# Gated linear attention: stacked gate product, halved state product, fewer decay operations

## The chip, the cores and the metric

The kernel runs on one core of a Trainium2 chip. The metric is the device time of one execution in microseconds (us).

## What is computed

One inference step of a hybrid decoder layer: 2048 prompt tokens and 8 single-token samples, model width 1024, all float32. Each token's normalised row is projected; one part goes through sliding-window attention, the other through gated linear attention (GLA), both are joined by an output product, and a SwiGLU network follows. The change touches the GLA part, which the reference gives as

```
log_a = log_sigmoid(u_lr @ w_gla_gate2 + b_gla_gate) / 16
b = cumsum(log_a)                                       # inside a chunk
o_inter = (q * exp(b)) @ S
scores[t, s] = sum_d q[t, d] * k[s, d] * exp(b[t, d] - b[s, d])   for s <= t
o = o_inter + scores @ v
S = exp(b_last) * S + (k * exp(b_last - b)).T @ v
g = rmsnorm(o) * silu(r)
```

with four heads of 64 key and 128 value channels, and a gate of rank 16.

## The kernel before

The program has three stages on one core: projections and window attention (to about 400 us of the profile), the GLA stage (about 400 to 740 us), then the output product and the network. A scheduler, run when the kernel is built, fixes the order of the instructions on each engine by a simulated timeline; at run time every engine takes its own list in order and waits on semaphores. Edits anywhere can thus move instructions of the whole program.

In the GLA stage tokens go in eight pairs of 128-token blocks. `front_b(pp)` loads the normalised tokens of a pair and projects q and k (`ps_qk`, L685) and v (`ps_v`, L728), each as three products of a high and a low float32r part (`mm3`, L104 to L106). Its `gates()` multiplies the 16 columns of the low-rank input `lrT` with `w2` in plain float32 (`ps_g`, L706; twice a pair), then ACT and DVE make the decay and its running sum `Bt`. `gla_b(pp)` computes the scores of a pair of blocks. The decay between two tokens is split over seven levels (64, 32, 16, 8, 4, 2, 1): at each level DVE subtracts the running sum at the middle of each section from the others, once for each half of the section (L785, L786), ACT takes the exponential (L787), POOL multiplies the later halves with q into the block-diagonal tile `bd` (four operations, L802), DVE the earlier halves with k (two, L803), and PE multiplies the two (`ps_l`, L807, four float32 products of 128 columns). The result is copied into `AT` under a mask (L815; level 64 without one, by ACT, L810). Then, per block, PE forms the output `po` from `AT` and v (L854) and from the state (L857), and the state's increment `pst` (L859): keys of two heads times values of two heads, 128 by 256, of which the two 64 by 128 diagonal parts are used. DVE updates the state `Sbd` (L867) and adds the diagonal to make `ob` (L873). ACT squares (L878), POOL takes the power for the reciprocal root (`rs_r`, L112), DVE multiplies `ob` by it and by the gate `r` in four column blocks (L882), PE transposes (`ps_m`, L886), ACT evicts, and SP stores to `mix_d` (L889), from where the output product reads it.

The scheduler mixes the projections of pair pp+1 between the level products of pair pp on PE. In the last pair nothing is left to mix in but the first tiles of the output product (`ps_wo`), whose inputs come by SP's queue too. Between the attention of the last block and the first `ps_v` PE needs the first gate product; in SP's queue the loads of `lrT` stand among the stores of the attention's outputs (L391, of tile `o`). DVE also splits `wro` into `wohl` for the output product in this stage (L763).

The lines to follow: L84 to L87 (constants), L325 to L327 (`lrT` leaves the first stage), L672 to L677 and L706 (gates), L778 to L816 (levels), L848 to L867 (outputs and state), L868 to L889 (scaling).

Of the kernel before, what the change touches and what calls it, by code (L numbers as in the profile page):

```python
# [20 lines left out]
P = 128  # L21
# [30 lines left out]
def hymba_kernel(ctx: ExitStack, tc: tile.TileContext, I, O, X=None, phases=3):  # L52
# [14 lines left out]
    lr_d = [dram.tile([16, 256], F32, name=f"lr_d{i}") for i in range(NB // 2)]  # L67
# [18 lines left out]
    w2 = const.tile([16, 256], F32, name="w2")  # L86
# [57 lines left out]
    with ExitStack() as ph:  # L144
# [140 lines left out]
        def project(b):  # L285
# [39 lines left out]
            lrT = wk.tile([16, P], F32, tag="lrT", name="lrT", bufs=1)  # L325
            nc.scalar.copy(lrT, ps[:16, 2 * P:3 * P])
            nc.sync.dma_start(lr_d[b // 2][:, (b % 2) * P:(b % 2 + 1) * P], lrT)  # L327
# [206 lines left out]
        for b in range(NB):  # L534
            if b + 2 < NB:
                front(b + 2)
            if 1 < b + 1 < NB:
                project(b + 1)
                if b + 1 < NB - 2:
                    project_r(b + 1)  # L540
            attend(b)
            if b >= 1:
                next(dec, None)
            if b == 3:
                nc.sync.dma_start(gg, I["gla_norm_g"].rearrange("o d -> d o"))
                nc.sync.dma_start(w2, I["w_gla_gate2"][0])
# [39 lines left out]
    with ExitStack() as ph:  # L586
# [67 lines left out]
        for i in range(2):  # L654
            AT = pc.tile([P, 4, 2, P], F32, name=f"AT{i}")
            nc.gpsimd.memset(AT, 0.0)
            ATs.append(AT)
        for i in range(3):
            bd = bdp.tile([P, 4, 2, 64], F32, name=f"bd{i}")
# [6 lines left out]
        def front_b(pp):  # L666
# [5 lines left out]
            lrT = qkp.tile([16, 264], F32, tag="lrT", name="lrTb")  # L672
            nc.sync.dma_start(lrT[:, 0:256], lr_d[pp])
            if pp == 0:
                nc.vector.tensor_copy(nT[:, 0, :, 256:264], nTdec[:, :, 0:ND])
                nc.vector.tensor_copy(nT[:, 1, :, 256:264], nTdec[:, :, 32:40])
                nc.vector.tensor_copy(lrT[:, 256:264], lrTdec)  # L677
# [15 lines left out]
            def gates():  # L693
# [8 lines left out]
                for p in range(2):  # L702
# [3 lines left out]
                    nc.tensor.matmul(ps[:, :W], w2[:, p * P:(p + 1) * P], lrT[:, :W], start=True, stop=True)  # L706
# [65 lines left out]
        def gla_b(pp):  # L772
# [5 lines left out]
            for li, H in enumerate(LEVELS):  # L778
                J = 64 // H
                E = wl.tile([P, 2, 256], F32, tag="E", name="E", bufs=3)  # L780
                Bv = Bt.rearrange("p a (n two o) -> p (a n) two o", two=2, o=H)
                Ev = E.rearrange("p a (n two o) -> p (a n) two o", two=2, o=H)
                G = 4 * J
                ref = Bv[:, :, 0, H - 1:H].to_broadcast([P, G, H])
# [11 lines left out]
                for p in range(2):  # L796
                    bv = bd[:, 2 * p:2 * p + 2].rearrange("p g h (j o) -> p g h j o", o=H)
                    for h in range(2):
                        rows = slice(64 * h, 64 * h + 64)
                        eo = E5[rows, p, :, 1].rearrange("p (c j) o -> p c j o", c=2)  # L800
                        qo = qv[rows, p, :, 1].rearrange("p (c j) o -> p c j o", c=2)
                        nc.gpsimd.tensor_tensor(bv[rows, :, h], eo, qo, ALU.mult)  # L802
                    nc.vector.tensor_tensor(E5[:, p, :, 0], E5[:, p, :, 0], kv[:, p, :, 0], ALU.mult)  # L803
                ps = lvp.tile([P, 512], F32, tag="lv", name="ps_l")
                Ef = E.rearrange("p a t -> p (a t)")
                for g in range(4):
                    nc.tensor.matmul(ps[:, g * P:(g + 1) * P], Ef[:, g * P:(g + 1) * P],  # L807
                                     bd[:, g].rearrange("p h t -> p (h t)"), start=True, stop=True)
                if H == 64:
                    nc.scalar.copy(AT[0:64].rearrange("p g h t -> p (g h) t")[:, :, 64:128],  # L810
                                   ps[0:64].rearrange("p (g t) -> p g t", t=64))
# [6 lines left out]
            qk = wl.tile([P, 2, 256], F32, tag="E", name="qk", bufs=3)  # L818
# [12 lines left out]
            kd = wl.tile([P, 2, 256], F32, tag="E", name="kd", bufs=3)  # L831
# [12 lines left out]
            for c in range(2):  # L844
# [4 lines left out]
                for p in range(2):  # L849
# [6 lines left out]
                    if b > 0:  # L856
                        nc.tensor.matmul(po[:, p * 256:(p + 1) * 256], eBf[:, g * P:(g + 1) * P], Sbd[:, p, :],  # L857
                                         start=False, stop=last, skip_group_check=True)
                    nc.tensor.matmul(pst[:, p * 256:(p + 1) * 256], kdN[:, g, :], v[:, p * 256:(p + 1) * 256],  # L859
                                     start=True, stop=True)  # L860
                for p in range(2):
                    g = 2 * p + c
                    for h in range(2):
                        rows = slice(64 * h, 64 * h + 64)
                        hc = slice(p * 256 + h * P, p * 256 + h * P + P)
                        sl = Sbd[rows, p, h * P:(h + 1) * P]
                        nc.vector.scalar_tensor_tensor(sl, sl, ebl[rows, g:g + 1], pst[rows, hc], ALU.mult, ALU.add)  # L867
# [8 lines left out]
                for hh in range(4):  # L876
                    hc = slice(hh * P, (hh + 1) * P)
                    nc.scalar.activation(osq, ob[:, hc], AF.Square, accum_out=ss[:, hh:hh + 1])  # L878
                rr = rstd(ss, P, 1.0 / P, 4)
                for hh in range(4):  # L880
                    hc = slice(hh * P, (hh + 1) * P)
                    nc.vector.scalar_tensor_tensor(ob[:, hc], ob[:, hc], rr[:, hh:hh + 1], r[:, hc], ALU.mult, ALU.mult)  # L882
                ps = aux.tile([P, 512], F32, tag="aux", name="ps_m")
                for hh in range(4):
                    hc = slice(hh * P, (hh + 1) * P)
                    nc.tensor.transpose(ps[:, hc], ob[:, hc], ident)  # L886
# [546 lines left out]
```

## Time and profile before

| | |
|---|---|
| median of 3 runs | 2298.53 us (2294.03 to 2301.5) |
| the profiled execution, its own time | 2301.44 us |
| its span, first to last instruction | 2299.7 us |
| PE busy with matmuls | 2223.9 us, 97% of the span, 12649 records |
| DVE, ACT, POOL busy | 1597.5 us (69%), 955.6 us (42%), 627.8 us (27%) |
| mean granted clock of PE | 0.984 of full speed |

An engine's busy time is the time in which at least one of its instructions runs. The records of PE overlap: the next starts while the end of the one before is still counted, so the cost of a matmul is read from the distance between two starts. A plain float32 matmul leaves two records, a float32r one or a transpose one. "Idle before" names the wait that ended last.

### The profile page before, as it was taken

The numbers are of one execution on the slowest core, as the hardware profiler recorded it, in microseconds if no ns is written. First come the engines' busy times: TensorE is split into PE (matmuls) and PEld (weight loads), VectorE is DVE, ScalarE is ACT, GpSimd is POOL, SyncE is SP. The second block draws the span as 40 slices with busy tenths as digits, with TensorE's granted clock in tenths as the row PEclk, the third lists the DMA queues.
The fourth block names the chain that finished last, engine by engine and source line by source line (L and its number), as shares of the span: only waits on it lengthen the run. The fifth ranks groups of instructions, "written<-read, shape, count | busy, mean of one in ns | idle before, by whom it ended". The sixth has DMA issues, their size and how long they took to land.

```text
span 2299.7 us, 34866 instructions
## 1 busy us (share of the span) xinstructions
PE 2223.9 (97%) x12649; PEld 1921.5 (84%) x12649; DVE 1597.5 (69%) x3241; ACT 955.6 (42%) x2121; POOL 627.8 (27%) x799
## 2 busy tenths in 40 slices
PE   8999998899998899999999999999999999999997
PEld 6888886788887788688888889999999968787886
DVE  6787887588676466766666767666676675748487
ACT  5666777343443233423333323333333243434342
POOL 2443443455465133311110111111010122222222
PEclk9999998999998999999999999999999999999999
DMA  7323334245424699863333357323232378878777
GB/s 240 122 77 111 94 102 157 92 138 171 143 88 184 237 293 317 303 202 110 92 112 94 103 186 277 98 88 107 87 115 88 106 212 174 218 168 218 166 206 239
DMA packets 211225, 364.35 MB, mean 158 GB/s; under 512 B 15428, under 2 KB 128349, under 8 KB 207965
## 3 DMA queue, kind: packets, MB, share of 16 engines
q1 hardware_dynamic: 173996, 258.65, 34.6%
q0 software_dynamic: 37056, 103.47, 17.7%
q8 instruction: 100, 1.64, 0.3%
q14 instruction: 73, 0.59, 0.1%
HBM read 210.98 MB, written 152.16 MB: 158 GB/s over the span
## 4 chain that ended last, share of the span: by engine, by line
PE 81%; DVE 5%; DMA 5%; issue 4%; POOL 2%; ACT 2%; SPq 0%; POOLq 0%; DVEq 0%; ACTq 0%
PE ps_b L105 7%; PE ps_b L104 7%; PE ps_b L106 7%; PE ps_c L105 5%; PE ps_c L104 5%; PE ps_c L106 5%; PE ps_a L105 5%; PE ps_a L104 5%; PE ps_a L106 5%; PE ps_d L104 3%; PE ps_wo L104 3%; PE ps_d L106 3%; PE ps_d L105 3%; PE ps_wo L106 3%; PE ps_wo L105 3%
## 5 line engine op out<-in xcount | busy, mean ns | idle before, releaser
L104 PE MATMUL ps_b<-z,whl 128*128 128x258 f32 (+1 forms) x792 | 254.0, 321 | 1.2 <-ACT whl L92 1.2
L106 PE MATMUL ps_b<-z,whl 128*128 128x258 f32 (+1 forms) x792 | 253.1, 320 | 1.7 <-DVE whl L93 1.7
L105 PE MATMUL ps_b<-z,whl 128*128 128x258 f32 (+1 forms) x792 | 254.3, 321 | 0.0
L92 ACT CAST dm<-mr 128x384 fp32r<-128x384 f32 (+1 forms) x224 | 108.1, 488 | 187.2 <-PE ps_b L106 99.4
L105 PE MATMUL ps_a<-z,whl 128*128 128x258 f32 (+1 forms) x528 | 169.2, 320 | 0.0
L105 PE MATMUL ps_c<-z,whl 128*128 128x258 f32 (+1 forms) x528 | 169.1, 320 | 0.0
L106 PE MATMUL ps_a<-z,whl 128*128 128x258 f32 (+1 forms) x528 | 168.9, 320 | 0.0
L106 PE MATMUL ps_c<-z,whl 128*128 128x258 f32 (+1 forms) x528 | 168.9, 320 | 0.0
L104 PE MATMUL ps_c<-z,whl 128*128 128x258 f32 (+1 forms) x528 | 168.6, 319 | 0.2 <-DMA z<-zc_d_P 0.2
L104 PE MATMUL ps_a<-z,whl 128*128 128x258 f32 (+1 forms) x528 | 168.8, 320 | 0.0
L106 PEld LDWEIGHTS ps_b<-z,whl 128*128 128x128 f32 x792 | 149.4, 189 | 14.5 <-DVE whl L93 2.4
L104 PEld LDWEIGHTS ps_b<-z,whl 128*128 128x128 f32 x792 | 149.4, 189 | 13.1 <-ACT whl L92 1.3
L105 PEld LDWEIGHTS ps_b<-z,whl 128*128 128x128 f32 x792 | 149.3, 189 | 11.9
L93 DVE TENSOR_TENSOR dm<-mr,dm 128x384 fp32r<-128x384 f32 (+1 forms) x224 | 115.1, 518 | 59.6 <-ACT dm L92 59.6
L92 ACT CAST whl<-wrg 128x512 fp32r<-128x512 f32 x132 | 81.6, 619 | 156.7 <-PE ps_b L106 82.2
L802 POOL TENSOR_TENSOR bd<-E,qTb 64x128 f32<-64x128 f32 x224 | 126.7, 566 | 60.7 <-ACT E L787 47.2
L969 DVE TENSOR_TENSOR gu<-ps_c,gu 128x512 f32<-128x512 f32 (+1 forms) x130 | 78.0, 600 | 57.8 <-PE ps_c L106 57.2
L93 DVE TENSOR_TENSOR whl<-wrg,whl 128x512 fp32r<-128x512 f32 x132 | 90.7, 688 | 36.6 <-ACT whl L92 36.3
L1268 POOL DMA_DIRECT2D md_d<-m x22 | 15.6, 711 | 363.8 <-DVE m L1231 363.8
L92 ACT CAST whl<-sy 128x512 fp32r<-128x512 f32 x88 | 54.6, 620 | 134.7 <-PE ps_b L106 84.7
L104 PE MATMUL ps_wo<-WO,mt 128*128 128x512 f32 x256 | 103.6, 404 | 6.9 <-ACT mt L92 6.9
L104 PEld LDWEIGHTS ps_c<-z,whl 128*128 128x128 f32 x528 | 99.8, 189 | 8.6 <-issue 0.6
(390 smaller groups left out, 6669.1 us busy)
## 6 DMA issues: line engine op xcount, KB each, us to landing
mr<-md_d SPq DMA_DIRECT2D x24, 1344.0 KB
zc_d_P<-zhl POOLq DMA_DIRECT2D x56, 512.0 KB, 6.4
z<-zc_d_P SPq DMA_DIRECT2D x14, 2048.0 KB
wrg<-in_w_gate_dram SPq DMA_DIRECT2D x44, 512.0 KB
wrg<-in_w_up_dram SPq DMA_DIRECT2D x44, 512.0 KB
nT_d<-nT SPq DMA_DIRECT2D x16, 1024.0 KB
zT<-nT_d SPq DMA_DIRECT2D x8, 2048.0 KB
h_d<-gu POOLq DMA_DIRECT2D x48, 256.0 KB, 4.6
```

Of the source, the lines that this page charges most:

```text
L92: nc.scalar.copy(h, src)
L93: (eng or nc.vector).tensor_tensor(l, src, h.bitcast(F32), ALU.subtract)
L104: nc.tensor.matmul(ps, lh, rh, start=start, stop=False, skip_group_check=more)
L105: nc.tensor.matmul(ps, lh, rl, start=False, stop=False, skip_group_check=more)
L106: nc.tensor.matmul(ps, ll, rh, start=False, stop=stop, skip_group_check=more)
L802: nc.gpsimd.tensor_tensor(bv[rows, :, h], eo, qo, ALU.mult)
L969: nc.vector.tensor_tensor(out, a, b, ALU.add)
L1268: nc.gpsimd.dma_start(md_d[sb][g][:, :, q, fp - GROUPS[g][0], :], src.rearrange("p (m t) -> p m t", m=4))
```

## The change

The gate product becomes one float32r product. `w3` holds 96 rows: the high part of `w2` in rows 0 to 15 and again in 32 to 47, the low part in 64 to 79, zeros elsewhere; `lr3` holds the high, low and high parts of the low-rank input in the same rows. The first stage stores both parts of `lrT`, and three loads fill `lr3`, one of two fixed tiles that POOL zeroes at the start of the GLA stage. The state increment becomes four products a block, of 64 key columns and 128 value columns each, written to the two halves of the PSUM partitions. At each level one subtraction covers both halves of a section, ACT takes the magnitude and then the exponential of its negative in a second operation; POOL multiplies with q in two operations instead of four, DVE with k in one instead of two; level 32 is copied by ACT without a mask, as level 64. POOL multiplies `ob` with `r`, and ACT scales the product by `rs_r`, in place of DVE's four operations. The tile E has four buffers instead of three.

```diff
-    lr_d = [dram.tile([16, 256], F32, name=f"lr_d{i}") for i in range(NB // 2)]
+    lr_d = [dram.tile([16, 2, 256], F32, name=f"lr_d{i}") for i in range(NB // 2)]
...
+    w3 = const.tile([96, 256], F32R, name="w3")
+    nc.gpsimd.memset(w3.bitcast(F32), 0.0)
...
-            nc.scalar.copy(lrT, ps[:16, 2 * P:3 * P])
-            nc.sync.dma_start(lr_d[b // 2][:, (b % 2) * P:(b % 2 + 1) * P], lrT)
+            split(lrT[:, 0], lrT[:, 1], ps[:16, 2 * P:3 * P])
+            nc.sync.dma_start(lr_d[b // 2][:, :, (b % 2) * P:(b % 2 + 1) * P], lrT.bitcast(F32))
...
+                split(w3[0:16], w3[64:80], w2)
+                nc.vector.tensor_copy(w3[32:48], w3[0:16].bitcast(F32))
...
+            lr3 = pad.tile([96, 264], F32R, name=f"lr3{i}")
+            nc.gpsimd.memset(lr3.bitcast(F32), 0.0)
...
-            lrT = qkp.tile([16, 264], F32, tag="lrT", name="lrTb")
-            nc.sync.dma_start(lrT[:, 0:256], lr_d[pp])
+            lr3 = lr3s[pp % 2]
+            for i, hl in enumerate((0, 1, 0)):
+                nc.sync.dma_start(lr3[32 * i:32 * i + 16, 0:256].bitcast(F32), lr_d[pp][:, hl])
...
-                    nc.tensor.matmul(ps[:, :W], w2[:, p * P:(p + 1) * P], lrT[:, :W], start=True, stop=True)
+                    nc.tensor.matmul(ps[:, :W], w3[:, p * P:(p + 1) * P], lr3[:, :W], start=True, stop=True)
...
-                nc.vector.tensor_tensor(Ev[:, :, 0], ref, Bv[:, :, 0], ALU.subtract)
-                nc.vector.tensor_tensor(Ev[:, :, 1], Bv[:, :, 1], ref, ALU.subtract)
-                grown = nc.scalar.activation(E, E, AF.Exp, scale=1.0 / 16)
+                E = wl.tile([P, 2, 256], F32, tag="E", name="E", bufs=4)
...
+                nc.vector.tensor_tensor(Ev, Bv, Bv[:, :, H - 1:H].to_broadcast([P, 4 * J, 2 * H]), ALU.subtract)
+                nc.scalar.activation(E, E, AF.Abs)
+                grown = nc.scalar.activation(E, E, AF.Exp, scale=-1.0 / 16)
...
-                for p in range(2):
...
-                        nc.gpsimd.tensor_tensor(bv[rows, :, h], eo, qo, ALU.mult)
-                    nc.vector.tensor_tensor(E5[:, p, :, 0], E5[:, p, :, 0], kv[:, p, :, 0], ALU.mult)
+                for h in range(2):
+                    rows = slice(64 * h, 64 * h + 64)
+                    nc.gpsimd.tensor_tensor(bv[rows, h], E5[rows, :, :, 1], qv[rows, :, :, 1], ALU.mult)
+                nc.vector.tensor_tensor(E5[:, :, :, 0], E5[:, :, :, 0], kv[:, :, :, 0], ALU.mult)
...
-                if H == 64:
...
+                if H >= 32:
+                    for j in range(J):
...
-                    nc.tensor.matmul(pst[:, p * 256:(p + 1) * 256], kdN[:, g, :], v[:, p * 256:(p + 1) * 256],
-                                     start=True, stop=True)
+                    for h in range(2):
+                        rows = slice(64 * h, 64 * h + 64)
+                        nc.tensor.matmul(pst[rows, p * P:(p + 1) * P], kdN[:, g, rows], v[:, (2 * p + h) * P:(2 * p + h + 1) * P],
+                                         start=True, stop=True)
...
+                nc.gpsimd.tensor_tensor(r, ob, r, ALU.mult)
                 rr = rstd(ss, P, 1.0 / P, 4)
...
-                    nc.vector.scalar_tensor_tensor(ob[:, hc], ob[:, hc], rr[:, hh:hh + 1], r[:, hc], ALU.mult, ALU.mult)
+                    nc.scalar.activation(r[:, hc], r[:, hc], AF.Copy, scale=rr[:, hh:hh + 1])
```

The scheduler then orders the instructions anew. Three places show it; a row is line, operation, output and inputs, size, and a count.

On SP, where the GLA stage starts (`mix_d` are the stores of the attention's last outputs, `lm` is the mask of the levels), before:

```order
L673 DMA lrTb<-lr_d_90 16x256
L391 DMA mix_d_86<-o 128x512
L673 DMA lrTb<-lr_d_91 16x256
L391 DMA mix_d_87<-o 128x512
L391 DMA mix_d_88<-o 128x512
L638 DMA lm<-in_c_lmask_dram 128x448
```

and with the change:

```order
L394 DMA mix_d_86<-o 128x512
L394 DMA mix_d_87<-o 128x512
L394 DMA mix_d_88<-o 128x512
L685 DMA lr_5008<-lr_d_89 16x256 x2
L644 DMA lm<-in_c_lmask_dram 128x448
L685 DMA lr_5008<-lr_d_89 16x256
```

The loads for the first gates (`lr_d_89`) stood two rows ahead of the first row shown; now they stand behind the last store.

On PE at the same place, with the change (L390 and L391 are the last attention products, L107 to L109 the three of `mm3`):

```order
L390 MATMUL po<-pT,vp_194 128x512
L391 MATMUL po<-pT,vp_194 128x512
L719 MATMUL ps_g<-lr_5008,w_130 128x264 x2
L107 MATMUL ps_v<-WV,zT 128x512
L108 MATMUL ps_v<-WV,zT 128x512
```

Before, the gate product stood ahead of the last eight attention products (L387, L388), with ten rows between it and the first `ps_v`; now it stands directly ahead of that.

On PE after the last level of the last pair, before:

```order
L807 MATMUL ps_l<-bd_4989,E 128x128 x4
L823 MATMUL ps_d<-hsel,qk 128x2 x4
L854 MATMUL po<-v,AT_4985 128x128 x2
L857 MATMUL po<-Sbd,eB 128x256
L854 MATMUL po<-v,AT_4985 128x128 x2
L857 MATMUL po<-Sbd,eB 128x256
L104 MATMUL ps_wo<-WO_8486,mt 128x512
```

and with the change:

```order
L816 MATMUL ps_l<-bd_5014,E 128x128 x4
L851 MATMUL ps_kd<-ident,kd 128x128 x4
L865 MATMUL po<-v,AT_5006 128x128 x2
L868 MATMUL po<-Sbd,eB 128x256
L865 MATMUL po<-v,AT_5006 128x128 x2
L868 MATMUL po<-Sbd,eB 128x256
L107 MATMUL ps_wo<-WO_8409,mt 128x512
```

The transposes of `kd`, on which the state's last updates rest, came after 18 products `ps_wo` and now come before all of them. The last transposes of the outputs (L886, now L900) are followed by 12 such products before, by 27 now, until the first product of the third tile.

## Rows read from the trace of the kernel before

**Rows 1.** Busy time by stretch: start:end, length; PE, PEld, DVE, ACT, POOL; clock, DMA.

```profile
425.00:720.00 295.00, 282.90 (x1839) 249.85 (x1838) 216.75 (x491) 120.01 (x289) 159.20 (x231) 0.99 0.37 118
720.00:742.00 22.00, 16.37 (x77) 15.07 (x76) 19.09 (x40) 6.73 (x17) 13.26 (x20) 0.61 1.02 408
```

**Rows 2.** Waits of PE, 425 to 756 us: in total, times, longest.

```profile
PE ps_l L807 <- POOL bd L802: 5.5, 14, 0.8
PE ps_l L807 <- DVE AT L815: 5.1, 3, 2.7
PE ps_l L807 <- DVE E L803: 4.4, 4, 2.3
```

**Rows 3.** Timeline of PE around a gate product: start, length, line, operation, tiles, shapes, count.

```profile
451.77 0.28 PE L105 MATMUL ps_qk<-zT,WQ 128*128 128x256 f32 x1
451.89 0.28 PE L106 MATMUL ps_qk<-zT,WQ 128*128 128x256 f32 x1
452.10 0.69 PE L706 MATMUL ps_g<-lrTb,w 16*128 16x256 f32 x2
452.72 1.13 PE L859 MATMUL pst<-v,kdN 128*128 128x256 f32 x4
```

**Rows 4.** Timeline of PE around a state product without a gate product.

```profile
711.70 1.02 PE L859 MATMUL pst<-v,kdN 128*128 128x256 f32 x4
712.37 0.58 PE L104 MATMUL ps_v<-WV,zT 128*128 128x512 f32 x1
712.79 0.39 PE L105 MATMUL ps_v<-WV,zT 128*128 128x512 f32 x1
```

**Rows 5.** Timeline of PE, level products of 128 columns.

```profile
716.95 1.06 PE L807 MATMUL ps_l<-bd,E 128*128 128x128 f32 x8
717.84 0.60 PE L857 MATMUL po<-Sbd,eB 128*128 128x256 f32 x2
```

**Rows 6.** Timeline of PE, products with 40 weight columns.

```profile
423.06 3.85 PE L734 MATMUL ps_v<-WV,nTdec 128*40 128x512 f32 x16
426.75 0.83 PE L807 MATMUL ps_l<-bd,E 128*128 128x128 f32 x6
```

**Rows 7.** DVE's groups by shape, 425 to 760 us: busy, mean ns, idle before.

```profile
L803 DVE TENSOR_TENSOR E<-E,kTb 128x128 f32<-128x128 f32 x106 | 39.2, 414 | 6.6 <-ACT E L787 5.9
L786 DVE TENSOR_TENSOR E<-Bt 128x256 f32<-128x256 f32 x53 | 30.3, 571 | 0.0
L785 DVE TENSOR_TENSOR E<-Bt 128x256 f32<-128x256 f32 x53 | 27.9, 527 | 2.1 <-POOL bd L802 1.5 <-issue 0.2
L882 DVE SCALAR_TENSOR_TENSOR ob<-ob,rs_r,r 128x128 f32<-128x128 f32 x60 | 23.8, 458 | 9.2 <-POOL rs_r L112 9.1
...
L833 DVE TENSOR_TENSOR kd<-Bt 128x512 f32<-128x512 f32 x8 | 6.0, 752 | 0.0
```

**Rows 8.** POOL's groups by shape, 425 to 760 us.

```profile
L802 POOL TENSOR_TENSOR bd<-E,qTb 64x128 f32<-64x128 f32 x213 | 120.9, 568 | 50.9 <-ACT E L787 38.1
...
L819 POOL TENSOR_TENSOR qk<-qTb,kTb 128x512 f32<-128x512 f32 x8 | 11.2, 1401 | 0.6
```

**Rows 9.** ACT's groups by shape, 425 to 760 us.

```profile
L787 ACT ACTIVATE E<-E 128x512 f32<-128x512 f32 x53 | 33.3, 630 | 63.7 <-DVE E L786 59.5 <-DVE rs_v L111 2.7 <-PE ps_qk L106 1.1
...
L708 ACT ACTIVATE la<-ps_g,nbT 128x256 f32<-128x256 f32 x14 | 6.6, 471 | 20.7 <-PE ps_g L706 20.7
```

**Rows 10.** Timeline of PE at the first `ps_v`.

```profile
410.43 0.80 PE L104 MATMUL ps_v<-WV,zT 128*128 128x512 f32 x1 [1.84 <-ACT Bt L709]
```

**Rows 11.** Timeline of SP at the same place.

```profile
403.41 6.88 SPq L391 DMA_DIRECT2D mix_d<-o  x2
410.35 0.42 SPq L638 DMA_DIRECT2D lm<-in_c_lmask_dram  x1
```

**Rows 12.** Timeline of DVE, the first reader of `lm`.

```profile
413.05 0.40 DVE L639 CAST lmask<-lm 128x448 uint8<-128x448 f32 x1 [2.24 <-DMA lm<-in_c_lmask_dram]
```

**Rows 13.** Timeline of PE at the end of the stage.

```profile
775.32 0.79 PE L104 MATMUL ps_wo<-WO,mt 128*128 128x512 f32 x1 [6.93 <-ACT mt L92]
```

More of the change, by code (lines that the diff above doesn't have):

```diff
@@ L324, in project @@
             nc.vector.scalar_tensor_tensor(kT[:, 1, :, P:], kp, gk, kT[:, 0, :, P:].bitcast(F32), ALU.mult, ALU.subtract)
-            lrT = wk.tile([16, P], F32, tag="lrT", name="lrT", bufs=1)
-            nc.scalar.copy(lrT, ps[:16, 2 * P:3 * P])
-            nc.sync.dma_start(lr_d[b // 2][:, (b % 2) * P:(b % 2 + 1) * P], lrT)
+            lrT = wk.tile([16, 2, P], F32R, tag="lrT", name="lrT", bufs=1)
+            split(lrT[:, 0], lrT[:, 1], ps[:16, 2 * P:3 * P])
+            nc.sync.dma_start(lr_d[b // 2][:, :, (b % 2) * P:(b % 2 + 1) * P], lrT.bitcast(F32))
             if b < NB - 1:
@@ L545, in hymba_kernel @@
                 nc.sync.dma_start(gg, I["gla_norm_g"].rearrange("o d -> d o"))
+                w2 = pc.tile([16, 256], F32, name="w2")
                 nc.sync.dma_start(w2, I["w_gla_gate2"][0])
+                split(w3[0:16], w3[64:80], w2)
+                nc.vector.tensor_copy(w3[32:48], w3[0:16].bitcast(F32))
                 for p in range(2):
@@ L657, in hymba_kernel @@
             ATs.append(AT)
+        lr3s = []
+        for i in range(2):
+            lr3 = pad.tile([96, 264], F32R, name=f"lr3{i}")
+            nc.gpsimd.memset(lr3.bitcast(F32), 0.0)
+            lr3s.append(lr3)
         for i in range(3):
-            bd = bdp.tile([P, 4, 2, 64], F32, name=f"bd{i}")
+            bd = bdp.tile([P, 2, 4, 64], F32, name=f"bd{i}")
             nc.gpsimd.memset(bd, 0.0)
@@ L676, in front_b @@
                 nc.vector.tensor_copy(nT[:, 1, :, 256:264], nTdec[:, :, 32:40])
-                nc.vector.tensor_copy(lrT[:, 256:264], lrTdec)
+                split(lr3[0:16, 256:264], lr3[32:48, 256:264], lrTdec)
+                nc.vector.tensor_copy(lr3[64:80, 256:264], lr3[0:16, 256:264].bitcast(F32))
             qT = qkp.tile([P, 2, 264], F32, tag="qT", name="qTb")
@@ L807, in gla_b @@
                     nc.tensor.matmul(ps[:, g * P:(g + 1) * P], Ef[:, g * P:(g + 1) * P],
[L808 to L811 removed]
+                                     bd[:, :, g], start=True, stop=True)
+                if H >= 32:
+                    for j in range(J):
+                        rows = slice(2 * H * j, 2 * H * j + H)
+                        nc.scalar.copy(AT[rows].rearrange("p g h t -> p (g h) t")[:, :, 2 * H * j + H:2 * H * j + 2 * H],
+                                       ps[rows].rearrange("p (g t) -> p g t", t=64)[:, :, H * j:H * j + H])
                 else:
@@ L816, in gla_b @@
                                               ps.rearrange("p (g j o) -> p g j o", g=8, o=H))
-            qk = wl.tile([P, 2, 256], F32, tag="E", name="qk", bufs=3)
+            qk = wl.tile([P, 2, 256], F32, tag="E", name="qk", bufs=4)
             nc.gpsimd.tensor_tensor(qk, qT[:, :, 0:256], k2, ALU.mult)
@@ L830, in gla_b @@
             nc.gpsimd.tensor_tensor(eB, eB, qT[:, :, 0:256], ALU.mult)
-            kd = wl.tile([P, 2, 256], F32, tag="E", name="kd", bufs=3)
+            kd = wl.tile([P, 2, 256], F32, tag="E", name="kd", bufs=4)
             Bc = Bt.rearrange("p a (c t) -> p (a c) t", t=P)
```

19 lines of the change are left out of this document (5 added, 14 removed).

## The prediction

> **What bounds the kernel now.** I read the page first: PE is busy for 97% of the span, so time is won where PE does less or waits less. The table of busy time by stretch then shows the stage that the change touches [rows 1]: for most of it (425 to 720 us) PE is busy 282.9 of 295 us and DVE, next, 216.8. In the 22 us after, when the projections have run out, PE falls to 16.4 us at a granted clock of 0.61 (most of that stretch at the lower level, 1.2 GHz, after PE had stood waiting) and DVE is the fullest engine with 19.1. PE's waits [rows 2] name the same partners: level products that wait for POOL's `bd`, DVE's `E` and `AT`, 15.0 us together. The two longest, 2.7 and 2.3 us, lie behind 720 us, so 10 are mid-stage, in 19 pieces. Last the timeline of PE, whose distances between starts give prices.
>
> **The gate product.** A float32r product of 256 columns costs 0.12 us (451.77 to 451.89) [rows 3]. The gate product takes 0.62 (452.10 to 452.72), its predecessor lasts 0.21 instead of 0.12, and the four records behind it take 1.13 instead of 1.02 [rows 3, 4]. That is 0.62 + 0.09 + 0.11 = 0.82 us; two records of 256 columns account for 0.43 of it (below), so 0.39 us go to entering and leaving a product of 16 weight rows. With 96 rows I take the plain price, 0.12. Fourteen of the sixteen stand amid PE work: 14 x 0.70 = **-9.8 us**. The first two stand beside waits and count nothing here.
>
> **The state product.** Four records of 256 columns and one of 512 take 1.09 us (711.70 to 712.79) [rows 4]; one record of 512 columns lasts 3.69 / 16 = 0.23 us [rows 6], so a record of 256 columns costs 0.215. A block has four, 0.86 us. Now it has eight of 128 columns, at (717.84 - 716.95) / 8 = 0.11 each [rows 5]: 0.88. So if the halves follow each other nothing changes: **0**. They use different columns of the array; if they ran side by side, half would go, 16 x 0.43 = 6.9 us. The other end is a charge on narrow products. Rows speak against it for few columns: sixteen products of 40 weight columns come at 0.23 each, and the next full product follows without a gap [rows 6]. But none of them writes the upper partitions, so both ends stay open.
> The Trainium skill, TensorE: Matmul & The Clock Gate, in its part on packing small matmuls, reports 2.38 times the speed for three products in different column groups; by that the term would lie near -6.9. No row here shows such an overlap.
>
> **The waits in mid-stage.** Per level DVE has now 0.57 + 0.53 + 2 x 0.41 = 1.92 us; then one subtraction of 512 columns, 0.75 (as L833), and one product of 256 columns, 0.53 (as L785): 0.64 less [rows 7]. DVE also loses L882, 4 x 0.46 = 1.83 us a block. POOL has 4 x 0.57 = 2.27 us a level; the new operation of 256 columns lies between 0.57 and the 1.40 of 512 columns, by width 0.85, so two take 1.70: 0.57 less [rows 8]. It gains one of 1.40 a block. ACT gains a magnitude a level, 0.63 [rows 9], 56 x 0.63 = 35 us in all, and 64 scalings of at most that; it stood at 120 of 295 us [rows 1], so it has room, but each level's chain grows by 0.63 where DVE and POOL take 1.2 out of it. A shorter chain should take away part of the 10 us. Ends: all of it, or none and 0.63 more for each of the 19 pieces, +12. I take half, **-5**, since a good part of these waits is on POOL, which gains least.
>
> **The last pair.** Of DVE's 19.1 busy us in the 22 us after 720 [rows 1], seven levels give back 7 x 0.64 and two blocks 2 x 1.83, together 8.1. POOL stands at 13.3 and changes by -7 x 0.57 + 2 x 1.40, so about 12: it does not fill the stretch either, and what is left is latency, with ACT's extra step in it. Ends 0 and -8.1; I take half, **-4**.
>
> **The end of the stage.** PE stands 6.93 us before the third tile of the output product [rows 13]: its input comes from ACT, which waits for a load that SP issues after the last block's store. With the change 27 instead of 12 products stand behind the last transposes, 15 x 0.23 = **-3.5**, provided the transposes' own input is not late; it has 41 such products (9.5 us) as cover. Ends 0 and -6.9.
>
> **The start of the stage.** This is the new wait. The first loads of `lr3` stand on SP behind the last attention store, which leaves at 410.3 [rows 11]. Two issues of about 0.4 us, `lm`, and the third come after it: issued at 411.6. `lm`, issued at 410.35, was there at 413.05 [rows 11, 12], 2.7 us; so the third lands at about 414.3. PE has the gate product, and behind it all of `ps_v`, which started at 410.43 [rows 10]: +3.9, and then ACT's first reads of the bank that `ps_v` needs, 2 x 0.47 [rows 9] and a hand-over. I take **+5**, ends +3.6 and +7. POOL's two new memsets come before that store and hide behind it.
>
> **Small things at nothing:** the split of `w2` on ACT and DVE and of `lrT` (in the first stage, one operation more on DVE a block) have the projections of the first stage around them; without that cover 16 operations at no more than the 0.41 of a 128 x 128 one [rows 7] would show, under 7 us. Sixteen more small loads on SP lie among its waits. The masked copy of level 32 goes from DVE to ACT.
>
> **The sum** is -9.8 + 0 - 5 - 4 - 3.5 + 5 = -17.3 us. Against the profiled execution's own 2301.4 that is 2284.1; that execution lies 2.9 us above the median of the three runs, 2298.5, from which I count: forecast **2281 us**.
>
> **Rivals.**
> (1) *More than that:* the halves overlap and the waits go to their ends: -9.8 - 6.9 - 10 - 8.1 - 6.9 + 5 = -37, 2262 us. For it: DVE gives up a quarter of its work. Against: the waits on POOL are short and many (14 of 0.4 us [rows 2]), which is the scheduler's order, not an overload.
> (2) *ACT's chain takes the place:* the three middle gains vanish, -9.8 + 5 = -4.8, 2294 us, with seven times 0.63 in the uncovered last pair 2298. For it: the magnitude sits in the chain of every level, and ACT's list also holds the copies that free PSUM for the projections. Against: PE waits for ACT nowhere in this stretch [rows 2].
> (3) *Narrow columns are charged when entered and left:* the new order visits the state product 27 times; at the gate product's 0.39 that is +10.5, 2292 us. The Trainium skill, TensorEngine Tiling (Array Packing), Key Properties, says that a change of tiling mode drains the engine, though a change of tile within a mode does not. By that rule this case holds; the 16-row rows agree with it, the 40-column rows [rows 6] do not.
> (4) *Slower:* each half is charged, since the partitions it writes change each time: 64 products at 0.39 is +25, and 2281 + 25 = 2306 us. It decides from 0.27 us per half on (17.3 / 64). Nothing in the trace shows a product that writes the upper half alone, which is all that speaks for it.
> (5) *The gate product keeps its charge* because 96 rows are not full either: 14 x 0.39 = +5.5, 2287 us.
>
> **Chances.** Forecast 0.50 (its own range 2273 to 2290), (1) 0.14, (2) 0.17, (3) 0.08, (4) 0.06, (5) 0.05. A measurement of this kernel tells about 0.3% from no change, 6.9 us: faster means below 2291.6, slower above 2305.4. Faster: nearly all of the forecast, (1), (5), and a part of (2) and (3): 0.74. Slower: (4), 0.06. The rest 0.20. The range 2263 to 2297 leaves out (4), the worse half of (2)'s ends and half of (1).
>
> **What would show it.** Right: gate products one record each at 0.12 with no wider distances around them; state records at 0.11 in a row; fewer waits of level products on `bd`, `E` and `AT`; DVE no longer the fullest engine in the last pair; PE idle some 5 us longer before the first `ps_v`, waiting for a DMA; the idle before the third output tile near 3.4 us. Wrong: distances of 0.2 us and more around the halves, waits of PE on ACT in mid-stage, or a first `ps_v` on time.

## The result and the profile after

The change took 2284.64 us (median of four runs, 2284.15 to 2286.41), the kernel before 2299.04 beside it: a ratio of 0.9932, 95% interval 0.9919 to 0.9946, or 14 us less. The forecast was 2281. The total came within 4 us of it; several of its terms did not, and two edits that gain together gain nothing apart.

Busy time by stretch in the kernel after (length; PE, PEld, DVE, ACT, POOL; clock, DMA), first two stretches of [rows 1]:

```profile
425.00:720.00 295.00, 278.07 (x1940) 246.48 (x1939) 201.20 (x354) 173.00 (x426) 171.73 (x161) 0.99 0.41 138
720.00:742.00 22.00, 20.92 (x109) 16.74 (x109) 10.25 (x22) 8.57 (x26) 5.83 (x5) 0.90 0.55 207
```

The stage now ends some 13 us earlier, so these stretches no longer hold the same work. I therefore cut by work: from the first `ps_v` to the start of the last level product, and from there to the third tile of the output product. Before:

```profile
410.43:735.88 325.45, 307.72 (x1946) 270.38 (x1946) 239.85 (x549) 131.92 (x316) 178.37 (x262) 0.97 0.40 132
735.88:775.32 39.44, 32.51 (x150) 27.18 (x150) 15.37 (x38) 8.84 (x24) 3.83 (x4) 0.89 0.46 176
```

and after:

```profile
413.34:723.12 309.78, 292.85 (x1995) 259.00 (x1996) 211.70 (x370) 182.41 (x445) 177.36 (x165) 0.98 0.41 138
723.12:757.77 34.65, 30.53 (x150) 23.73 (x149) 11.78 (x28) 10.77 (x31) 5.13 (x5) 0.98 0.49 182
```

The first stretch lost 15.7 us, the second 4.8, while the first `ps_v` starts 2.9 later; what follows is equal within 0.4 us. That is the 17.2 us between the spans, 2299.7 and 2282.5. In the first stretch PE is busy 14.9 us less, but its idle time (length less busy) only fell from 17.7 to 16.9. The waits of PE, 425 to 756 us, answer to [rows 2]:

```profile
PE po L865 <- DVE AT L826: 5.7, 5, 1.7
PE ps_l L816 <- POOL bd L811: 5.7, 7, 2.2
PE ps_m L900 <- ACT r L896: 3.4, 1, 3.4
PE ps_l L816 <- DVE AT L826: 1.6, 1, 1.6
PE ps_l L816 <- issue: 1.2, 1, 1.2
```

They changed their partners and hardly their sum. [rows 2] has the three longest of five rows of its view; with the two short ones left out there the sum was 16.7 us, and here, with a sixth row of 0.2, it is 17.8. The wait of level products on `E` is gone, an output product waits for `AT`, and a transpose for ACT's scaling.

The timeline of PE around a gate product, as [rows 3]: one record, 0.12 us to the next start, and a predecessor at 0.12 as well.

```profile
453.01 0.28 PE L109 MATMUL ps_qk<-zT,WQ 128*128 128x256 f32 x1
453.13 0.28 PE L719 MATMUL ps_g<-lr,w 96*128 96x256 f32 x1
453.25 0.61 PE L865 MATMUL po<-v,AT 128*128 128x128 f32 x4
```

The state product in halves, as [rows 4], once with eight records and once with four:

```profile
450.94 0.28 PE L107 MATMUL ps_qk<-zT,WQ 128*128 128x256 f32 x1
451.14 0.66 PE L873 MATMUL pst<-v,kdN 128*64 128x128 f32 x8
451.73 0.39 PE L108 MATMUL ps_qk<-zT,WQ 128*128 128x256 f32 x1
451.96 0.28 PE L109 MATMUL ps_qk<-zT,WQ 128*128 128x256 f32 x1
...
496.32 0.38 PE L868 MATMUL po<-Sbd,eB 128*128 128x256 f32 x1
496.63 0.44 PE L873 MATMUL pst<-v,kdN 128*64 128x128 f32 x4
497.00 0.71 PE L865 MATMUL po<-v,AT 128*128 128x128 f32 x4
497.55 0.60 PE L868 MATMUL po<-Sbd,eB 128*128 128x256 f32 x2
```

Eight records take 0.59 us where one after the other they would take 0.88, so the halves run side by side. But the product ahead takes 0.20 instead of 0.12, and the one behind 0.23 instead of 0.12: 0.78 in all, 0.57 for four by the same count. Four records more cost 0.21, and what is left, 0.36, is charged on the visit. The other visits that stand amid PE work agree: 0.56 to 0.57 us for those with four records, 0.78 to 0.79 for those with eight. The full products before show no such charge, 0.43 us for two records and 0.86 for four where no gate product is near. There are 28 visits in the trace with 128 records: 28 x 0.36 + 128 x 0.053 = 16.9 us, against 64 x 0.215 = 13.8 before.

The start of the stage on PE (the first row after the last attention product), and on SP, as [rows 10, 11]:

```profile
405.67 0.40 PE L391 MATMUL po<-pT,vp 128*128 128x512 f32 x1
411.54 0.78 PE L719 MATMUL ps_g<-lr,w 96*128 96x264 f32 x2 [5.47 <-DMA lr<-lr_d]
413.34 0.79 PE L107 MATMUL ps_v<-WV,zT 128*128 128x512 f32 x1 [1.02 <-ACT Bt L722]
```

```profile
400.28 7.47 SPq L394 DMA_DIRECT2D mix_d<-o  x2
407.84 0.84 SPq L685 DMA_DIRECT2D lr<-lr_d  x2
408.78 0.37 SPq L644 DMA_DIRECT2D lm<-in_c_lmask_dram  x1
409.20 0.42 SPq L685 DMA_DIRECT2D lr<-lr_d  x1
```

The third load is issued 1.4 us behind the last store, and PE stands for it: 7.67 us between the last attention product and the first `ps_v`, where there were 2.24.

DVE's and POOL's groups by shape, 425 to 760 us, as [rows 7, 8]:

```profile
L797 DVE TENSOR_TENSOR E<-Bt 128x512 f32<-128x512 f32 x52 | 43.0, 860 | 9.8 <-issue 5.5 <-POOL bd L811 2.4 <-PE ps_l L816 1.4
...
L812 DVE TENSOR_TENSOR E<-E,kTb 128x256 f32<-128x256 f32 x53 | 35.5, 680 | 15.6 <-ACT E L799 15.2
```

```profile
L811 POOL TENSOR_TENSOR bd<-E,qTb 64x256 f32<-64x256 f32 x109 | 100.6, 923 | 28.5 <-DVE E L797 13.7 <-PE ps_l L816 5.4 <-ACT E L799 3.2
```

Fewer operations saved less than I had by width: a level costs DVE 0.86 + 0.68 = 1.54 us, so 0.38 less (I had 0.64), and POOL 2 x 0.92 = 1.85, 0.43 less (0.57).

The end of the stage on PE and SP, as [rows 13]: the idle before the third tile fell from 6.93 to 3.05.

```profile
757.77 0.50 PE L107 MATMUL ps_wo<-WO,mt 128*128 128x512 f32 x1 [3.05 <-ACT mt L95]
```

```profile
749.27 0.33 SPq L903 DMA_DIRECT2D mix_d<-mob  x1
749.78 0.84 SPq L1021 DMA_DIRECT2D h<-in_x_prompt_dram  x2
750.71 0.38 SPq L1016 DMA_DIRECT2D mr<-mix_d  x1
```

The load `mr` of the third tile stands behind the stage's last store in SP's list.

### The profile page after: what moved, and what is told of

Its sections match the earlier page's. It is cut to its first block, busy times and chain, and to the rows that moved or that the text cites. A ratio compares the mean times of both kernels' runs of the same rounds, so it can differ in the third digit from the quotient of the medians.

```text
span 2282.5 us, 34902 instructions
## 1 busy us (share of the span) xinstructions
PE 2206.6 (97%) x12697; PEld 1908.8 (84%) x12697; DVE 1567.7 (69%) x3076; ACT 1009.3 (44%) x2259; POOL 625.3 (27%) x706
## 3 DMA queue, kind: packets, MB, share of 16 engines
q1 hardware_dynamic: 174764, 259.05, 34.7%
q0 software_dynamic: 37056, 103.47, 17.8%
## 4 chain that ended last, share of the span: by engine, by line
PE 82%; DMA 5%; DVE 5%; issue 3%; POOL 2%; ACT 2%; SPq 0%; POOLq 0%; DVEq 0%; ACTq 0%
PE ps_b L108 8%; PE ps_b L107 8%; PE ps_b L109 8%; PE ps_c L108 5%; PE ps_c L107 5%; PE ps_c L109 5%; PE ps_a L108 5%; PE ps_a L107 5%; PE ps_a L109 5%; PE ps_d L107 3%; PE ps_d L108 3%; PE ps_d L109 3%; PE ps_wo L107 3%; PE ps_wo L109 3%; PE ps_wo L108 2%
## 5 line engine op out<-in xcount | busy, mean ns | idle before, releaser
L109 PE MATMUL ps_b<-z,whl 128*128 128x258 f32 (+1 forms) x792 | 253.6, 320 | 2.1 <-DVE whl L96 2.1
L107 PE MATMUL ps_b<-z,whl 128*128 128x258 f32 (+1 forms) x792 | 254.3, 321 | 1.2 <-ACT whl L95 1.2
L109 PE MATMUL ps_a<-z,whl 128*128 128x258 f32 (+1 forms) x528 | 169.2, 320 | 0.0
L109 PE MATMUL ps_c<-z,whl 128*128 128x258 f32 (+1 forms) x528 | 169.1, 320 | 0.0
L107 PE MATMUL ps_c<-z,whl 128*128 128x258 f32 (+1 forms) x528 | 168.9, 320 | 0.2 <-DMA z<-zc_d_P 0.2
L107 PE MATMUL ps_a<-z,whl 128*128 128x258 f32 (+1 forms) x528 | 169.0, 320 | 0.0
L109 PEld LDWEIGHTS ps_b<-z,whl 128*128 128x128 f32 x792 | 149.6, 189 | 14.5 <-DVE whl L96 2.5
L107 PEld LDWEIGHTS ps_b<-z,whl 128*128 128x128 f32 x792 | 149.7, 189 | 13.0 <-ACT whl L95 1.3
L811 POOL TENSOR_TENSOR bd<-E,qTb 64x256 f32<-64x256 f32 x112 | 103.2, 922 | 44.3 <-DVE ebl L840 15.7
L1282 POOL DMA_DIRECT2D md_d<-m x22 | 15.6, 711 | 363.5 <-DVE m L1245 363.5
L107 PEld LDWEIGHTS ps_c<-z,whl 128*128 128x128 f32 x528 | 100.0, 189 | 8.5 <-issue 0.6
L107 PEld LDWEIGHTS ps_a<-z,whl 128*128 128x128 f32 x528 | 100.0, 189 | 7.9
```

What stands on the lines that cost most here:

```text
L107: nc.tensor.matmul(ps, lh, rh, start=start, stop=False, skip_group_check=more)
L109: nc.tensor.matmul(ps, ll, rh, start=False, stop=stop, skip_group_check=more)
L811: nc.gpsimd.tensor_tensor(bv[rows, h], E5[rows, :, :, 1], qv[rows, :, :, 1], ALU.mult)
L1282: nc.gpsimd.dma_start(md_d[sb][g][:, :, q, fp - GROUPS[g][0], :], src.rearrange("p (m t) -> p m t", m=4))
```

## The experiments

Each is measured beside the kernel before on the same chip, in four groups: the medians of the kernel before were 2300.8 (the first four below), 2299.7 (from state_grouped to levels_no_scaling), 2301.1 (scaling_alone, third_tile_early, v_two_products) and 2300.5 (sums_early). Ratios are to these. The table gives each kernel's median, the time from the last attention product to the first `ps_v` (A), from there to the last level product (B), PE's idle in B (its length less PE's busy time), and from there to the third output tile (C). They are read from the timelines and stretches as above. The last attention product starts at 403 to 408 us in all of them, and what follows the third tile takes 1523 to 1527 us, 1529 in gates_alone. The stretches come from one execution of each kernel, up to 4 us from its median, so differences of 2 or 3 us between rows decide nothing by themselves.

An edit also moves other instructions, since the scheduler orders anew. I compare the sequence of PE's records from the first `ps_v` to the third output tile, the edited products left out. In loads_early (against the change), third_tile_early (against grouped_early) and sums_early (against third_tile_early) under 1% of the other records stand in another place. In each of the remaining experiments it is 11 to 26%, 16% in gates_alone. So three experiments change one thing only; the others change the order too.

| kernel | median us | A | B | idle in B | C |
|---|---|---|---|---|---|
| before | 2299.0 | 2.2 | 325.4 | 17.7 | 39.4 |
| gates_alone | 2303.5 | 8.1 | 320.8 | 22.4 | 40.9 |
| halves_alone | 2302.8 | 2.2 | 323.6 | 20.0 | 42.4 |
| levels_no_scaling | 2304.8 | 4.9 | 320.7 | 21.3 | 44.2 |
| scaling_alone | 2302.7 | 2.2 | 325.8 | 18.4 | 41.6 |
| levels_alone (with the scaling) | 2284.7 | 4.9 | 314.4 | 11.0 | 32.4 |
| full_state | 2286.6 | 7.9 | 314.9 | 15.5 | 34.4 |
| the change | 2284.6 | 7.7 | 309.8 | 16.9 | 34.7 |
| state_grouped | 2284.7 | 7.8 | 304.8 | 16.2 | 39.6 |
| loads_early | 2280.5 | 2.2 | 311.0 | 17.5 | 35.2 |
| grouped_early | 2280.7 | 2.2 | 309.5 | 17.9 | 37.1 |
| third_tile_early | 2279.4 | 2.2 | 309.8 | 19.6 | 34.3 |
| sums_early | 2272.2 | 2.2 | 309.2 | 17.7 | 29.9 |
| v_two_products | 2257.1 | 2.2 | 287.0 | 21.8 | 34.7 |

**gates_alone**: of the change only `w3`, `lr3` and what feeds them.

```diff
-nc.tensor.matmul(ps[:, :W], w2[:, p * P:(p + 1) * P], lrT[:, :W], start=True, stop=True)
+nc.tensor.matmul(ps[:, :W], w3[:, p * P:(p + 1) * P], lr3[:, :W], start=True, stop=True)
```

> The kernel before with the stacked gate product alone. In this kernel too the loads of lr3 stand on SP behind the last attention store. Theory: 14 gate products amid PE work cost 0.12 instead of 0.82 us, -9.7, and PE waits 5.4 us longer ahead of the first ps_v (the change showed 6.5 against 1.84 idle there): about 2299 - 4 = 2295. Rival: the time of the gate product is not its own, and goes to its neighbours: 2299 + 5 = 2304.

2303.5, ratio 1.0009 (0.9996 to 1.0022): no gain. The price was right:

```profile
413.05:733.89 320.84, 298.44 (x1931) 266.01 (x1932) 239.94 (x544) 130.33 (x316) 175.62 (x262) 0.97 0.40 132
```

PE is busy 9.3 us less than before in B. But it is idle 4.7 us more there, so that B is 4.6 shorter; A, where the same edit brings the late loads, is 5.8 us longer and C 1.5. So the rival's reason falls, though its 2304 came out: the price did not go to the neighbours of the product. The theory of 2295 misses the idle time in B.

**halves_alone**: only the state product in halves.

```diff
-nc.tensor.matmul(pst[:, p * 256:(p + 1) * 256], kdN[:, g, :], v[:, p * 256:(p + 1) * 256], start=True, stop=True)
+for h in range(2):
+    nc.tensor.matmul(pst[rows, p * P:(p + 1) * P], kdN[:, g, rows], v[:, (2 * p + h) * P:(2 * p + h + 1) * P], start=True, stop=True)
```

> The kernel before with the state product in column halves alone; its order visits the state product 24 times (8 times with 8 records, 16 times with 4). Theory A, from the trace of the change: two halves run side by side (0.11 us a pair of records instead of 0.215 a record, -6.9 us in all), and each visit is charged 0.35 us for entering and leaving (+8.4): about +1.5, 2300.5. Theory B, side by side without a charge: 2292. Theory C, a charge on each half: over 2310.

2302.8, ratio 1.0014 (1.0004 to 1.0024): theory A's small loss; theories B and C are out. The row of the table does not show the loss where theory A has it: PE is busy 4.0 us less in B than before, at a granted clock of 0.98 instead of 0.97, and C is 2.9 longer.

**levels_alone**: the edits of levels and output scaling.

```diff
-nc.vector.tensor_tensor(Ev[:, :, 0], ref, Bv[:, :, 0], ALU.subtract)
-nc.vector.tensor_tensor(Ev[:, :, 1], Bv[:, :, 1], ref, ALU.subtract)
+nc.vector.tensor_tensor(Ev, Bv, Bv[:, :, H - 1:H].to_broadcast([P, 4 * J, 2 * H]), ALU.subtract)
+nc.scalar.activation(E, E, AF.Abs)
...
-nc.vector.scalar_tensor_tensor(ob[:, hc], ob[:, hc], rr[:, hh:hh + 1], r[:, hc], ALU.mult, ALU.mult)
+nc.scalar.activation(r[:, hc], r[:, hc], AF.Copy, scale=rr[:, hh:hh + 1])
```

> The kernel before with the edits of the levels and of the output scaling alone (one subtraction and a magnitude on ACT, fewer products, E with four buffers, POOL's product with r, ACT's scaling); gates and state product as before. Forecast's terms: waits in mid-stage -5, last pair -4, end of stage -3.5: 2286.5. Theory from the trace of the change: PE's idle time between the first ps_v and the last transposes stays within 2 us of before's 17.7, and the gain is the clock in the last pair (about -6) and the end of the stage (-3 to -4): 2289 to 2290. Rival, ACT's longer chain takes the place: 2299 or more.

2284.7, ratio 0.9933 (0.9918 to 0.9948): the whole gain of the change, and more than any theory gave. My theory from the trace falls: idle in B went to 11.0, and C to 32.4. Rival "ACT's longer chain" is out as a net effect; what the longer chain costs by itself no run shows, and a transpose does wait 3.1 us for ACT's scaling here. A is 2.6 longer without any new load: the attention ends 2.6 us earlier than in the trace of before and the first `ps_v` starts at the same time, since ACT's `Bt` waits 2.51 us for a store of the attention (`mix_d`).

```profile
410.45:724.82 314.37, 303.37 (x1954) 270.25 (x1954) 210.72 (x371) 180.73 (x445) 177.73 (x165) 0.97 0.40 133
724.82:757.25 32.43, 29.49 (x144) 24.03 (x142) 12.51 (x27) 10.73 (x31) 6.78 (x6) 1.00 0.62 226
```

**full_state**: the change with the state product of before.

```diff
-for h in range(2):
-    nc.tensor.matmul(pst[rows, p * P:(p + 1) * P], kdN[:, g, rows], v[:, (2 * p + h) * P:(2 * p + h + 1) * P], start=True, stop=True)
+nc.tensor.matmul(pst[:, p * 256:(p + 1) * 256], kdN[:, g, :], v[:, p * 256:(p + 1) * 256], start=True, stop=True)
```

> The change with the state product of before (256 columns, both off-diagonal parts computed). Theory A: the halves cost 17.4 us where the full products cost 13.8, so this is 3.5 us faster than the change: about 2281. Theory B, the halves side by side are a net gain: up to 6.9 slower than the change, 2291. Forecast: no difference, 2284.6.

2286.6, ratio 0.9942 (0.9927 to 0.9957): its interval holds the change's ratio, so the total does not decide. What PE should save on the products did not arrive:

```profile
414.62:729.56 314.94, 299.45 (x1940) 270.33 (x1941) 212.86 (x370) 179.54 (x445) 179.09 (x165) 0.96 0.42 138
```

B is 5.2 us longer than in the change, at a granted clock of 0.96 instead of 0.98; 2% of 300 us is 6 us, by estimate all of it. The profiled execution lies 2.5 us above the kernel's median, and the order differs (18% of the records), so this run neither confirms nor refutes the price of the halves.

**state_grouped**: the halves of both blocks of a pair in one visit.

```diff
+pstb = pstp.tile([P, 4, P], F32, tag="pst", name="pst")
+for g in (0, 2, 1, 3):
+    for h in range(2):
+        rows = slice(64 * h, 64 * h + 64)
+        nc.tensor.matmul(pstb[rows, g], kdN[:, g, rows], vs[g % 2][:, (g // 2 * 2 + h) * P:(g // 2 * 2 + h + 1) * P], start=True, stop=True)
 for c in range(2):
```

> The change with the eight half products of a block pair issued together, ahead of the outputs, into one PSUM tile for both blocks: 8 visits of 16 records instead of 28 of 2 to 8. Theory A, a charge of 0.35 us a visit and halves side by side: 20 x 0.35 = -7 against the change, 2277.5, or less where waits on the levels take part of it back, 2281. Theory B, the cost does not hang on visits: 2284.6, as the change.

Sixteen records in one visit cost 1.03 + 0.09 + 0.10 = 1.22 us:

```profile
449.89 0.28 PE L107 MATMUL ps_qk<-zT,WQ 128*128 128x256 f32 x1
450.10 1.09 PE L859 MATMUL pst<-v,kdN 128*64 128x128 f32 x16
451.13 0.39 PE L108 MATMUL ps_qk<-zT,WQ 128*128 128x256 f32 x1
451.35 0.28 PE L109 MATMUL ps_qk<-zT,WQ 128*128 128x256 f32 x1
```

With the 0.78 of eight that is 0.055 a record and 0.34 a visit: the charge holds, the eight visits come to 8 x 1.22 = 9.8 us. Theory A was right on the price and wrong on the time, 2284.7, ratio 0.9931 (0.9917 to 0.9946): B lost 5.0 us and C gained 4.9. In the new order fewer output products stand behind the last transposes (9 instead of 27), and PE is idle 7.1 us in C instead of 4.1, at a lower clock:

```profile
717.77:757.36 39.59, 32.48 (x163) 27.04 (x162) 12.40 (x28) 13.14 (x36) 5.75 (x6) 0.89 0.48 177
```

**loads_early**: the two `lr3` tiles in the pool where `lrTb` had been.

```diff
-lr3 = pad.tile([96, 264], F32R, name=f"lr3{i}")
+lr3 = qkp.tile([96, 264], F32R, name=f"lr3{i}", bufs=1)
```

> The change with the two lr3 tiles in another pool, in whose place their zeroing and loads need not wait for the end of the attention: in SP's order the first loads now stand ahead of the last three attention stores, and on PE the first gate product stands ahead of the last attention products, as before. Theory: the 5.5 us that the gate product waited for its load go, PE's idle time ahead of the first ps_v falls from 6.5 to about 1.8, and a few more visits of the state product cost about 1: 2281. Rival: the loads for the third pair wait for PE's gate product and hold the stores behind them on SP, nothing is won: 2284.6.

2280.5, ratio 0.9916 (0.9899 to 0.9934), 4 us less than the change, as expected. The interval just holds the change's ratio, so the total alone does not decide; stretch A does, 2.2 instead of 7.7 us in nearly the same order, while B and C are 1.2 and 0.5 longer. The rival, nothing won, is unlikely.

```profile
405.28 0.40 PE L391 MATMUL po<-pT,vp 128*128 128x512 f32 x1
407.52 0.80 PE L107 MATMUL ps_v<-WV,zT 128*128 128x512 f32 x1 [1.84 <-ACT Bt L722]
```

**grouped_early**: both edits.

```diff
+pstb = pstp.tile([P, 4, P], F32, tag="pst", name="pst")
...
+lr3 = qkp.tile([96, 264], F32R, name=f"lr3{i}", bufs=1)
```

> Both of the last two together. If the start wait and the visit charges are separate and nothing gives them back: 2284.6 - 4.7 - 7 = 2273. If the levels' own pace gives back half of the visit charges: 2276.5. If the levels set the pace altogether: 2280.

2280.7, ratio 0.9914 (0.9898 to 0.9929): nothing over the early loads alone, and the case "the levels set the pace altogether" has the number. Its reason is not shown: B is 1.5 us shorter and C 1.9 longer, and the third tile waits 7 us.

```profile
753.82 0.80 PE L107 MATMUL ps_wo<-WO,mt 128*128 128x512 f32 x1 [6.97 <-ACT mt L95]
```

**levels_no_scaling** and **scaling_alone** split levels_alone: the first leaves the output scaling as it was, the second has only that.

```diff
+nc.gpsimd.tensor_tensor(r, ob, r, ALU.mult)
...
+nc.scalar.activation(r[:, hc], r[:, hc], AF.Copy, scale=rr[:, hh:hh + 1])
```

> The kernel before with the edits of the levels alone; the outputs are scaled by DVE as before. Levels and scaling together gave 2284.7. Theory A, the levels' shorter chain is what PE waited for: 2288, most of the gain. Theory B, the gain came from DVE's freed time after the levels (four scalings a block): 2296 or more.

> The kernel before with the output scaling alone (POOL's product with r, ACT's four scalings a block); levels, gates and state product as before. The levels alone gave 2304.8, both together 2284.7. Theory A, the two together: DVE must be freed on both sides before the last pair gets shorter, the scaling alone stays near 2297, with more than 38 us from the last level product to the third tile of the output product (before 39.4, both together 32.4). Theory B, the scaling alone is the gain: 2285.

2304.8, ratio 1.0023 (1.0013 to 1.0032), and 2302.7, 1.0009 (0.9998 to 1.0020): neither gains alone, the levels alone lose 5 us, together they gain 16. "Levels alone are most of the gain" falls, and so does "the scaling alone"; "the two together" holds. In levels_no_scaling the last transposes stand directly ahead of the third tile, so nothing covers the way over SP:

```profile
767.05 0.60 PE L884 MATMUL ps_m<-ident,ob 128*128 128x128 f32 x4
777.14 0.80 PE L104 MATMUL ps_wo<-WO,mt 128*128 128x512 f32 x1 [9.50 <-ACT mt L92]
```

In levels_alone 34 products stand there, and the idle is 1.7:

```profile
757.25 0.50 PE L104 MATMUL ps_wo<-WO,mt 128*128 128x512 f32 x1 [1.74 <-ACT mt L92]
```

That accounts for 8 of the 20 us between the two; B makes another 6. Whether DVE's freed time does it or the order that the scheduler then finds (22% of PE's records stand elsewhere) was not tried.

**third_tile_early**: grouped_early, and the inputs of the third and fourth output tile beside those of the first two.

```diff
-if ti in tiles[:2]:
-    mr = ztile(tiles.index(ti), "mr").rearrange("p s k t -> p (s k t)")[:, :1024].bitcast(F32)
+if ti in tiles[:4]:
+    i = tiles.index(ti)
+    if i < 2:
+        mrz.append(ztile(i, "mr").rearrange("p s k t -> p (s k t)").bitcast(F32))
+    mr = mrz[i % 2][:, 1024 * (i // 2):1024 * (i // 2) + 1024]
```

> The grouped state product with early lr3 loads (2280.7), and the inputs of the third and fourth tile of the output product put beside those of the first two, in memory that is free early: on SP their loads now stand ahead of the last three stores of the outputs, where they stood behind the last one. The third tile is block 1, which the last stores don't write. Theory: PE's 7.0 us of idle before the third tile go, with some of the low clock behind it: 2272. Rival: the wait is on the stage's last outputs or on another resource and only moves: 2280.

2279.4, ratio 0.9903 (0.9888 to 0.9918): the rival. The wait on `mt` went; another stood behind it, for DVE's sum that frees the PSUM bank and that waits for `h` in the same queue:

```profile
751.04 0.50 PE L107 MATMUL ps_wo<-WO,mt 128*128 128x512 f32 x1 [4.19 <-DVE h L586]
```

```profile
750.30 1.29 DVE L586 TENSOR_TENSOR h<-ps_wo,h 128x512 f32<-128x512 f32 x2 [1.11 <-DMA h<-in_x_prompt_dram]
```

**sums_early**: that, and `h` of the first two tiles early too.

```diff
-h = cu.tile([P, D], F32, tag="hl", name="h")
+if ti not in tiles[:2]:
+    h = cu.tile([P, D], F32, tag="hl", name="h")
...
+    if i < 2:
+        h = mrz[i][:, 2048:3072]
```

> The kernel with the third tile's load early (2279.4), and the residual rows h of the first two tiles of the output product also put in memory that is free early, so that their loads stand ahead of the last stores on SP too. There PE's wait before the third tile was 4.2 us, for DVE's sum of h and the product, which frees the PSUM bank and had waited for that load. Theory: the wait goes, 2275. Rival: the third tile then waits for something else on the same queue, or the saving comes back elsewhere as low clock: 2278 to 2279.5.

2272.2, ratio 0.9874 (0.9858 to 0.9891): 12 us less than the change and the fastest of the kernels that form all products. PE goes into the third tile without a gap, and C is 29.9, of which PE is busy 29.6 at a clock of 1.00:

```profile
747.38 0.39 PE L109 MATMUL ps_wo<-WO,mt 128*128 128x512 f32 x1
747.61 0.39 PE L107 MATMUL ps_wo<-WO,mt 128*128 128x512 f32 x1
```

**v_two_products**: loads_early with two of the three products for the prompt's values.

```diff
-mm3(ps, nT[:, 0, k, c0:c0 + n], nT[:, 1, k, c0:c0 + n], WV[:, 0, k], WV[:, 1, k], k == 0, k == KD - 1)
+for hl in range(2):
+    nc.tensor.matmul(ps, nT[:, 0, k, c0:c0 + n], WV[:, hl, k], start=k == 0 and hl == 0, stop=k == KD - 1 and hl == 1)
```

> The change with early lr3 loads (2280.5), and the values of the prompt's blocks projected with two of the three products: the low part of the input is left out there, 128 products of 0.23 us, 29.4 us of PE work less. Theory A, PE's work sets the pace of the stage: 2251. Theory B, the levels' chain on DVE, ACT and POOL sets the pace where PE has less to do, and work taken from PE comes back as waits and low clock, as with the gates (9.7 us less work, no gain) and the grouped state product (8 us less, no gain): 2266 to 2280.

2257.1, ratio 0.9812 (0.9796 to 0.9828), 23 us less than loads_early:

```profile
405.45:692.40 286.95, 265.14 (x1867) 235.41 (x1868) 220.30 (x375) 177.51 (x445) 180.96 (x165) 0.97 0.48 161
```

In loads_early:

```profile
407.52:718.54 311.02, 293.53 (x1995) 259.44 (x1996) 213.65 (x375) 182.23 (x445) 178.45 (x165) 0.97 0.42 141
```

PE is busy 28.4 us less in B and idle 4.3 more. So PE does set the pace, nearer to theory A: eight tenths of what it saves arrive. Some 4 us came back as waits, as many as with the gates, where they were half of the saving.

## Why the prediction was right, and where not

**What bounds the kernel**: right, with a limit. PE's work decides the stage (v_two_products), but not all that it saves arrives: with 9.3 us less work (gates_alone) PE was idle 4.7 us more. The sum treated the gate products as lying wholly on the path. My reading is that PE's products also cover the levels' chain. It is not shown: gates_alone changed the order as well, and in state_grouped PE is busy 4.3 us less in B than in the change and idle 0.7 less.

**Gate product, -9.8**: its price was right (one record at 0.12 amid PE work, -9.3 busy in gates_alone), what it is worth was not: only 4.6 us arrive in B, and the late start that comes with the same edit takes more than that, so alone it gains nothing.

**State product, 0**: this step failed. It took "if the halves follow each other nothing changes" between two open ends. Both ends came true at once: the halves overlap (0.053 to 0.055 us a record instead of 0.11), and each visit is charged 0.34 to 0.36. With 28 visits that is 16.9 us instead of 13.8, +3. The rows that I weighed against a charge, products of 40 columns without a gap, did not tell: their records read 128\*40, these 128\*64. Why the one shape is charged and the other not stays open; so does whether the 64 columns or the upper partitions draw the charge, since every visit has both. The Trainium skill, TensorE: Matmul & The Clock Gate, in its part on packing small matmuls, has products in different column groups running at once; the 16 records in 1.03 us agree. The Trainium skill, TensorEngine Tiling (Array Packing), Key Properties, has a change of tiling mode drain the engine; the 0.36 us on entering and leaving agree. Each page stands by one rival ((1) and (3)), and the truth was the sum of their two prices.

**Waits in mid-stage, -5, and the last pair, -4**: right for the edits they were made for, and not for the change. With levels and scaling alone idle in B fell by 6.7, the first part of the last pair's waits among it, and C by 7.0. In the change idle in B fell by 0.8 and C by 4.8. What failed is the step that took half of each wait as the share of these edits, to be added whatever the other edits do. The reason given, the shorter chain of a level, is not enough either: without the scaling the same shorter chain loses 5 us, and the scaling alone gains nothing. Together they gain 16. Gates, halves and levels with scaling, each alone, add up to about -10 us by their ratios, the change gave 15.6; with intervals of some 3 us on each, that is no clear difference. Two sizes were off as well: DVE gave up 0.38 us a level, not 0.64, and POOL 0.43, not 0.57.

**End of stage, -3.5**: measured -3.9 (6.93 to 3.05), by the mechanism named. That what is left is SP's order and no dependence on the last block shows in third_tile_early and sums_early, with the rest of the order nearly the same.

**Start, +5**: measured +5.4 (2.24 to 7.67 from the last attention product to the first `ps_v`), by the mechanism named, and loads_early takes it away. The span shows only +2.9 of it, since the attention ended 2.5 us earlier in that execution; without these 2.5 the two profiled executions differ by 14.7 us, as the medians do (14.4).

**The total** is right in part by luck, because misses offset one another: the state product cost 3 more than its term, the waits gave less in B, and PE's busy time fell further than gates and state explain (14.9 less, with 9.8 - 3 = 7 from these). At a clock of 0.98 instead of 0.97 in B, 1% of 300 us or 3 us of the rest is, by estimate, the clock; the remaining 5 stay open. Rival (4), slower, is out: a charge per half would have cost 64 times, and it falls on visits.

## What to carry to other kernels

Where one engine is busy for most of a stage, read busy and idle time of the same piece of work, since a saving may come back as a wait. Where a scheduler orders anew after every edit, an edit alone is not one change: compare the order before giving an edit the credit. Half-width products cost less than full ones only where many of them stand together. And look at what stands in a queue ahead of a late load: here four inputs that depended on nothing late stood behind a late store, and moving them was worth 8 us by the medians of grouped_early and sums_early, 6 by their spans (2278.9 and 2272.6), where the gate product and the halves alone gave nothing.

## What was not expected of the hardware

Two products of 64 columns that write different halves of the PSUM partitions run side by side (16 records of 128 columns in 1.03 us), and a group of them costs about 0.35 us on entering and leaving among full-width products, whether it holds 4, 8 or 16 records. The overlap saves 0.056 us a record (0.11 less 0.054), so by estimate a group pays from seven records on. A subtraction of DVE on 512 columns took 0.86 us on average in this stage, where the one I priced it by had taken 0.75 [rows 7]. The average hides two groups: 35 of the 52 took 0.66 to 0.71 us and 17 took 0.82 to 1.79. All 17 overlap an operation of POOL for most of their time, but so do some of the 35, so what lengthens them is not shown.
